# Where a decoder layer turns token-major tiles into feature-major ones: TensorE transposes, or VectorE blocks and a DMA round trip

## The chip, the cores and the metric

One core of one Trainium2 chip runs the whole kernel. The metric is the device time of one execution in microseconds (us). In the text PE is TensorE, DVE is VectorE, ACT is ScalarE, POOL is GpSimd and SP is SyncE; POOL and SP also issue DMAs, and each engine works through its own instructions in order.

## What is computed

One decoder layer on x of 256 tokens x 2048 features in float32: a half-step SwiGLU FFN (hidden width 5632), a token mixer of a gated linear attention branch (4 heads) and a dilated sliding-window attention branch (3 groups of 8 heads), merged by sigmoid gates, and a second half-step FFN. Each is modulated by shift, scale and gate rows made from a conditioning vector, and closed by a LayerNorm:

```python
f1 = swiglu(modulate(x, sh1, sc1), w_ffn1_gu[l], w_ffn1_down[l])
x = layer_norm(DN_ALPHA * x + 0.5 * g1[:, None, :] * f1, ln1_g[l], ln1_b[l])
m = hybrid_mixer(modulate(x, sh2, sc2), positions, w_in[l], w_alpha2[l], b_alpha[l],
                 gla_norm_g[l], w_branch_a[l], w_branch_b[l], w_out[l])
x = layer_norm(DN_ALPHA * x + g2[:, None, :] * m, ln2_g[l], ln2_b[l])
f2 = swiglu(modulate(x, sh3, sc3), w_ffn2_gu[l], w_ffn2_down[l])
x = layer_norm(DN_ALPHA * x + 0.5 * g3[:, None, :] * f2, ln3_g[l], ln3_b[l])
```

with, at the end of `hybrid_mixer`,

```python
y_a = o_a @ w_branch_a
...
y_b = o_b.reshape(B, S, DIL_OUT).astype(h.dtype) @ w_branch_b
merged = jax.nn.sigmoid(gate_a) * y_a + jax.nn.sigmoid(gate_b) * y_b
return merged @ w_out
```

Every product needs its left operand with the features on the partitions, while the products before it leave tokens on the partitions. So each intermediate is transposed in between.

## The kernel before

**Products.** A `Chunk` is one 512-column piece of a product for both token tiles (128 tokens each). It is cut into `Unit`s of two k-tiles (256 rows of the weight). `load` (L204) brings 4 k-tiles of a weight (1 MB, `raw`, three buffers) by SP; `split` (L209) casts a unit's part on ACT to float32r (`wh`), and `split_lo` (L220) subtracts on DVE to get the low half `wl`. `emit` (L235) issues, for both token tiles and both k-tiles, the three matmuls of `mm3` (high x high, high x low, low x high; L231 to L233) into a PSUM accumulator `acc`, 12 matmuls a unit. After a chunk's last unit it starts the chunk's `done` generator for each tile.

**The order of the work** is written out at build time. The loop at L1330 goes through all units: it splits the unit `SA` = 3 ahead, starts the generators due there, emits the unit, lets every side task of `Flow` do one step, and runs the conditioning reductions (`ada_step`, DVE, L382) up to a pace. `yield n` in a side task waits n steps. If `emit` needs a left operand whose task isn't through, `Flow.until` (L96) steps the tasks without emitting units until it is. Small SBUF tiles of 256 KB (`sml`) come from a pool of eight and are counted by `n_sml`; PSUM scratch tiles by `n_mps`.

**Left operands** are `Lhs` objects: groups kg of four feature tiles, a high and a low half, 256 tokens wide. `tok_to_lhs` (L551) fills one group for one token tile: after `wait` steps it takes a PSUM tile and makes four 128x128 transposes on PE (`transpose4`, L414), and a step later ACT copies the result to the high half (L402) and DVE subtracts to get the low half (L406). It is called

- for the FFN's hidden groups (`up_tail`, L574, wait 4): FFN1 in parts of 6 and 5 chunks, FFN2 in parts of 4, 4 and 3, each part followed by its down product, which reads the groups in order. FFN1's part 0 is "pieced": its product over the 16 k-tiles runs in five phases with partial sums in SBUF (L596, L602, L606),
- for the four heads of the linear attention (`gr_sink`, L994, into `oaT`),
- for both halves of the attention output (`lane`, L1163, into `obT`),
- for the four merged pieces (`mg_sink`, L1193, into `mT`, read by `w_out`). This sink loads `mg` from DRAM by POOL (L1198), multiplies (L1199), and adds two steps later (L1202); its chunks have four units each. `reload` (L1210) brings x back from DRAM by POOL, 1 MB per tile, at the first unit of `w_out`.

`qk_sink` (L1080) applies the rotary embedding to a q or k chunk on DVE (L1089 to L1094), transposes it on PE in the same way (L1098), and ACT copies it to `qkT` (L1101).

POOL does little else than issue DMAs: the bias rows of the conditioning, `x` for the first residual (L623), `gn`, `lng`, `lnb`, `spill`, `mgd`, `mg`.

Of the kernel before, what the change touches and what calls it, by code (L numbers as in the profile page):

```python
# [10 lines left out]
F32 = mybir.dt.float32  # L11
# [5 lines left out]
P = 128  # L17
D = 2048
S = 256
# [126 lines left out]
def layer(ctx, tc, a):  # L146
# [401 lines left out]
            yield  # L548


    def tok_to_lhs(src, lhs, kg, t, wait=2):  # L551
        yield wait
        ps = yield from mps([P, 4, P])
        transpose4(ps, src, 0)
        yield
        put_split(lhs, kg, t, ps)
        n_mps.give()

    def ffn(w_gu, w_dn, X, gm, ln, norm, parts, pieced):
# [13 lines left out]

        def up_tail(t, sg, hT, kg):  # L574
            s = sg[t]
            yield from tok_to_lhs(s, hT, kg, t, 4)
            n_sml.give()

        def up_sink(c, sg, hT, kg):
            def done(t, ps):  # L580
# [80 lines left out]

        for pi, part in enumerate(parts):
            hT = Lhs(fl)
            if pi == 0 and pieced:
                sgs = {c: [None, None] for c in part}
                for q, (k0, nk) in enumerate(PHASES):
                    if nk == 2:
                        for c in part[::2]:
                            for e in range(2):
                                it = Item(w_gu, k0 * P, e * DFF + c * NC5, True)  # L670
                                items.append(it)
                                for i in range(2):
                                    Chunk(w_gu, 0, 0, 2, X, pieced_sink(c + i, e, q, sgs[c + i], hT, c + i),
                                          k0=k0, wide=(it, i))
                    else:
                        for c in part:
                            for e in range(2):
                                Chunk(w_gu, k0 * P, e * DFF + c * NC5, nk, X,
                                      pieced_sink(c, e, q, sgs[c], hT, c), k0=k0)
            else:  # L680
                for c in part:
                    sg = [None, None]
                    kg = c - part[0]
                    Chunk(w_gu, 0, c * NC5, KD, X, gate_sink(c, sg), head=pi == 0 and c == 0)
                    Chunk(w_gu, 0, DFF + c * NC5, KD, X, up_sink(c, sg, hT, kg))
            for n in range(4):
                Chunk(w_dn, part[0] * NC5, n * NC5, 4 * len(part), hT, down_sink(pi, n), tail=pi == last and n == 3)
# [306 lines left out]
    def gr_sink(h):  # L994
# [3 lines left out]
        def done(t, ps):  # L998
            s = yield from sml(name="gr")
            A_.activation(s, ps, AF.Silu)  # L1000
            n_acc.give()
            while ("o", hh, t) not in g:
                yield
            o = g["o", hh, t]
            V.tensor_mul(o, o, s)
            n_sml.give()
            yield from tok_to_lhs(o, oaT, h, t)
            n_sml.give()
        return done

    def starter(gen, units_from):
# [65 lines left out]
    def att_set(hs4):  # L1077
        d = dict(qk={}, v={}, n=0, ob=[None, None], left=[4, 4])

        def qk_sink(which, g):  # L1080
            def done(t, ps):
# [11 lines left out]
                n_acc.give()  # L1093
                V.tensor_add(r1, r1, r2)  # L1094
                n_sml.give()
                yield 4
                pt = yield from mps([P, 4, P])
                transpose4(pt, r1.rearrange("p h e d -> p (h e d)"), 0)  # L1098
                n_sml.give()
                yield  # L1100
                A_.copy(dst[:, :, t * P:(t + 1) * P], pt)  # L1101
                n_mps.give()
                d["n"] += 1
            return done

# [57 lines left out]
        def lane(t):  # L1163
# [4 lines left out]
                yield from job(j, t)  # L1168
            while max(d["left"]):
                yield  # L1170
            yield from tok_to_lhs(d["ob"][t], obT, hs4, t)
            n_sml.give()

        for which, off in ((0, OFF_DQ), (1, OFF_DK)):
            for g in range(3):
# [17 lines left out]
    def mg_sink(n):  # L1193
        sl = slice(n * NC5, (n + 1) * NC5)

        def done(t, ps):
# [1 line left out]
            nc.gpsimd.dma_start(mg, mgd[t][:, sl])  # L1198
            V.tensor_mul(sgb[t][:, sl], sgb[t][:, sl], ps)  # L1199
            n_acc.give()  # L1200
            yield 2
            V.tensor_add(mg, mg, sgb[t][:, sl])  # L1202
            yield from tok_to_lhs(mg, mT, n, t)
            n_sml.give()
        return done

    for n in range(4):
# [161 lines left out]
```

## Time and profile before

| | us |
|---|---|
| median of 3 runs | 2717.61 (2717.35 to 2717.94) |
| profiled execution, its own time | 2717.02 |
| span of its profile | 2715.2 |
| PE busy / DVE / ACT / POOL | 2646.8 / 1925.1 / 1201.0 / 42.8 |
| mean granted clock of PE | 0.996 |

The page gives the busy time of each engine over the span, the chain of work that ended last, and the costliest groups of instructions. A busy share says how much an engine does, not whether it sets the end: that is read from the chain, from what an engine waited for, and from stretches of the span. The matmuls of one engine overlap: the record of one is 0.39 us long, and the next starts before it ends, so costs on PE are read from start to start.

### The profile page before, as it was taken

The page shows a single profiled execution, that of the slowest core. Times are in us where ns is not written, and L with a number is a line of the kernel's source. Part 1 is how long each engine was busy: PE and PEld are TensorE (multiplying, and loading weights), DVE is VectorE, ACT ScalarE, POOL GpSimd, SP SyncE. Part 2 cuts the span into 40 slices and gives each one's busy share as a digit, 9 for nine tenths or more (in the row PEclk, how much of TensorE's full clock was granted, in tenths as well). Part 3 has the DMA queues.
Part 4 walks back from the last instruction along what each step waited for, and adds up shares of the span by engine and source line. Part 5 has one row for each costly group of instructions (what it writes and reads, how often), then busy time and mean ns, then how long its engine had stood idle before and what let it go on. Part 6 is the DMA issues. An engine that isn't in the chain of part 4 may idle for free.

```text
span 2715.2 us, 31195 instructions
## 1 busy us (share of the span) xinstructions
PE 2646.8 (97%) x12043; PEld 2180.4 (80%) x12043; DVE 1925.1 (71%) x2436; ACT 1201.0 (44%) x1387; POOL 42.8 (2%) x71
## 2 busy tenths in 40 slices
PE   6899999999999999999999999999999999999997
PEld 5678788888877788888888888888788888888886
DVE  8999977877876786676666676668766655655556
ACT  5333444444345544444544344554454444443443
POOL 0000000000000000000000000000000000000001
PEclk9999999999999999999999999999999999999999
DMA  9787798888855686666657667577567666656553
GB/s 377 268 315 274 240 325 309 304 286 291 279 194 178 230 286 221 217 232 233 216 202 256 240 233 243 194 239 257 199 217 255 226 230 235 225 186 212 207 186 124
DMA packets 327044, 654.23 MB, mean 241 GB/s; under 512 B 13128, under 2 KB 21552, under 8 KB 325616
## 3 DMA queue, kind: packets, MB, share of 16 engines
q1 hardware_dynamic: 322352, 633.46, 67.0%
q0 software_dynamic: 4544, 18.79, 2.1%
q8 instruction: 94, 1.54, 0.2%
q14 instruction: 54, 0.44, 0.0%
HBM read 645.90 MB, written 6.29 MB: 240 GB/s over the span
## 4 chain that ended last, share of the span: by engine, by line
PE 87%; DVE 9%; issue 2%; ACT 1%; DMA 1%; SPq 0%; DVEq 0%; ACTq 0%
PE acc L233 27%; PE acc L232 27%; PE acc L231 27%; DVE wl L225 3%; DVE part L382 2%; PE mps L416 2%; DVE part L596 1%; PE mps L1152 1%; PE mps L1124 1%; DVE lhs L406 1%; DVE xm L424 0%; PE mps L962 0%; ACT wh L215 0%; DMA abig<-in_w_ada 0%; PE mps L1141 0%
## 5 line engine op out<-in xcount | busy, mean ns | idle before, releaser
L225 DVE TENSOR_TENSOR wl<-raw,wh 128x1024 fp32r<-128x1024 f32 x912 | 1113.3, 1223 | 697.5 <-ACT wh L215 696.1
L215 ACT CAST wh<-raw 128x1024 fp32r<-128x1024 f32 x912 | 957.4, 1053 | 1306.6 <-PE acc L233 1242.4
L231 PE MATMUL acc<-wh,lhs 128*128 128x512 f32 x3648 | 1440.0, 395 | 12.0 <-DVE part L596 7.1
L232 PE MATMUL acc<-wl,lhs 128*128 128x512 f32 x3648 | 1423.8, 390 | 5.0 <-DVE wl L225 4.9
L233 PE MATMUL acc<-wh,lhs 128*128 128x512 f32 x3648 | 1424.0, 390 | 4.6 <-DVE lhs L406 4.6
L231 PEld LDWEIGHTS acc<-wh,lhs 128*128 128x128 f32 x3648 | 686.6, 188 | 158.9 <-ACT lhs L402 7.0
L233 PEld LDWEIGHTS acc<-wh,lhs 128*128 128x128 f32 x3648 | 686.2, 188 | 150.8 <-DVE lhs L406 6.3
L232 PEld LDWEIGHTS acc<-wl,lhs 128*128 128x128 f32 x3648 | 686.6, 188 | 149.8 <-DVE wl L225 8.7
L382 DVE SCALAR_TENSOR_TENSOR part<-araw,cact,part 128x512 f32<-128x512 f32 x432 | 320.3, 742 | 0.4
L382 DVE SCALAR_TENSOR_TENSOR part<-abig,cact,part 128x512 f32<-128x512 f32 x119 | 88.1, 747 | 3.2 <-DMA abig<-in_w_ada 1.6
L596 DVE TENSOR_TENSOR part<-part,acc 128x512 f32<-128x512 f32 x72 | 46.0, 680 | 0.0
L406 DVE TENSOR_TENSOR lhs<-mps,lhs 128x512 fp32r<-128x512 f32 x64 | 41.3, 682 | 1.6 <-ACT lhs L402 1.6
L402 ACT CAST lhs<-mps 128x512 fp32r<-128x512 f32 x64 | 34.4, 585 | 0.0
L1127 DVE TENSOR_TENSOR sS<-mps,consts 128x128 f32<-128x128 f32 (+1 forms) x48 | 16.0, 358 | 15.0 <-PE mps L1124 14.5
L570 ACT ACTIVATE sg<-acc 128x512 f32<-128x512 f32 x32 | 19.0, 598 | 16.0 <-PE acc L233 16.0
L604 ACT ACTIVATE sg<-sg 128x512 f32<-128x512 f32 x12 | 7.4, 633 | 40.2 <-DVE sg L602 40.2
L406 DVE TENSOR_TENSOR lhs<-xm,lhs 128x256 fp32r<-128x256 f32 (+1 forms) x34 | 17.6, 531 | 9.2 <-ACT lhs L402 8.5
L416 PE MATMUL mps<-ident,sg 128*128 128x128 f32 x176 | 22.8, 272 | 0.0
L416 PEld LDWEIGHTS mps<-ident,sg 128*128 128x128 f32 x176 | 20.5, 140 | 2.8
L416 PE MATMUL mps<-ident,part 128*128 128x128 f32 x96 | 15.1, 281 | 7.6 <-DVE part L382 7.3
L368 POOL DMA_DIRECT2D part<-in_b_ada x12 | 5.9, 493 | 1030.8 <-DVE part L382 433.3
L1143 ACT COPY pT<-mps 128x384 f32<-128x384 f32 x24 | 10.7, 480 | 24.2 <-PE mps L1141 24.2
(221 smaller groups left out, 875.0 us busy)
## 6 DMA issues: line engine op xcount, KB each, us to landing
raw<-in_w_ffn_gu SPq DMA_DIRECT2D x176, 1024.0 KB, 4.9
raw<-in_w_in SPq DMA_DIRECT2D x152, 1024.0 KB, 4.8
araw<-in_w_ada SPq DMA_DIRECT2D x224, 512.0 KB, 5.3
raw<-in_w_ffn_down SPq DMA_DIRECT2D x88, 1024.0 KB, 5.0
abig<-in_w_ada SPq DMA_DIRECT2D x24, 1024.0 KB, 7.5
raw<-in_w_branch_a SPq DMA_DIRECT2D x16, 1024.0 KB, 5.1
raw<-in_w_out SPq DMA_DIRECT2D x16, 1024.0 KB, 6.6
raw<-in_w_branch_b SPq DMA_DIRECT2D x8, 1024.0 KB, 5.0
```

Source lines behind the costliest of these rows:

```text
L215: A_.copy(wh, r)
L225: V.tensor_sub(wl, r, wh.bitcast(F32))
L231: T.matmul(ps, lhsT=xh, rhs=wh, start=first, stop=False)
L232: T.matmul(ps, lhsT=xh, rhs=wl, start=False, stop=False)
L233: T.matmul(ps, lhsT=xl, rhs=wh, start=False, stop=last)
L382: V.scalar_tensor_tensor(pt, w, cact[:, k:k + 1], pt, op0=ALU.mult, op1=ALU.add)
L402: A_.copy(hs, src)
L406: V.tensor_sub(b[:, 1, j, t * P:(t + 1) * P], src, b[:, 0, j, t * P:(t + 1) * P].bitcast(F32))
L416: T.transpose(ps[:, j], src[:, c0 + j * P:c0 + (j + 1) * P], ident)
L596: V.tensor_add(p, p, ps)
L1124: T.matmul(ps[:, 0:nk], lhsT=qk[g][:, 0, j, t * P:(t + 1) * P], rhs=qk[g][:, 1, j, 0:nk], start=True, stop=True)
L1152: T.matmul(ops[:, 0:HD], lhsT=pTs[kb][:, g], rhs=d["v"][g][:, kb, j * HD:(j + 1) * HD], start=i == 0, stop=i == n_mm - 1)
```

## The change

A new helper `turn` makes the transpose without PE. DVE transposes the 16 blocks of 32x32 of each 128x128 tile in one instruction into a small tile `s`; four DMAs from POOL write it to a DRAM tile `turned`, each 32 partitions wide, in runs of 512 bytes, so that the blocks end up at the right places; a fifth DMA, three steps later, reads it back whole (128 rows of 2 KB) into a small tile. Three steps after that the result is used. `tok_to_lhs_dma` is `tok_to_lhs` with `turn`: ACT copies the high half and DVE subtracts the low half, now from SBUF.

It takes the place of `tok_to_lhs` for all hidden groups of an FFN part but the last, for the heads of `oaT`, for the first half of `obT` and for the first three pieces of `mT`; `qk_sink` calls `turn` too. The others stay on PE. In `mg_sink` the addition comes four steps after the product instead of two.

```diff
--- before.py
+++ after.py
@@ -548,6 +548,36 @@
             yield
 
 
+    def turn(src, wait, give):
+
+
+        yield wait
+        s = yield from sml(name="turn")
+        V.transpose(s.rearrange("p (b k j) -> p b k j", b=4, k=4), src.rearrange("p (k b j) -> p b k j", k=4, b=4))
+        if give:
+            n_sml.give()
+        d = dr.tile([P, NC5], F32, tag="turn", name="turned", bufs=6)
+        dv = d.rearrange("(b i) (a x) -> a i b x", b=4, a=4)
+        for a4 in range(4):
+            nc.gpsimd.dma_start(dv[a4], s[32 * a4:32 * a4 + 32].rearrange("i (b x) -> i b x", b=4))
+        yield 3
+        n_sml.give()
+        o = yield from sml(name="turned")
+        nc.gpsimd.dma_start(o, d)
+        yield 3
+        return o.rearrange("p (a k j) -> p k a j", a=4, k=4)
+
+    def tok_to_lhs_dma(src, lhs, kg, t, wait=1, give=True):
+        o = yield from turn(src, wait, give)
+        if kg not in lhs.tiles:
+            lhs.tiles[kg] = blk([P, 2, 4, S], F32R, name="lhs")
+        hi, lo = (lhs.tiles[kg][:, e, :, t * P:(t + 1) * P].rearrange("p k (a j) -> p k a j", a=4) for e in range(2))
+        A_.copy(hi, o)
+        V.tensor_sub(lo, o, hi.bitcast(F32))
+        lhs.ready.update(((2 * kg, t), (2 * kg + 1, t)))
+        n_sml.give()
+
+
     def tok_to_lhs(src, lhs, kg, t, wait=2):
         yield wait
         ps = yield from mps([P, 4, P])
@@ -573,8 +603,11 @@
 
         def up_tail(t, sg, hT, kg):
             s = sg[t]
-            yield from tok_to_lhs(s, hT, kg, t, 4)
-            n_sml.give()
+            if kg < hT.last:
+                yield from tok_to_lhs_dma(s, hT, kg, t)
+            else:
+                yield from tok_to_lhs(s, hT, kg, t, 4)
+                n_sml.give()
 
         def up_sink(c, sg, hT, kg):
             def done(t, ps):
@@ -661,6 +694,7 @@
 
         for pi, part in enumerate(parts):
             hT = Lhs(fl)
+            hT.last = len(part) - 1
             if pi == 0 and pieced:
                 sgs = {c: [None, None] for c in part}
                 for q, (k0, nk) in enumerate(PHASES):
@@ -1004,8 +1038,7 @@
             o = g["o", hh, t]
             V.tensor_mul(o, o, s)
             n_sml.give()
-            yield from tok_to_lhs(o, oaT, h, t)
-            n_sml.give()
+            yield from tok_to_lhs_dma(o, oaT, h, t)
         return done
 
     def starter(gen, units_from):
@@ -1093,13 +1126,9 @@
                 n_acc.give()
                 V.tensor_add(r1, r1, r2)
                 n_sml.give()
-                yield 4
-                pt = yield from mps([P, 4, P])
-                transpose4(pt, r1.rearrange("p h e d -> p (h e d)"), 0)
+                o = yield from turn(r1.rearrange("p h e d -> p (h e d)"), 1, True)
+                A_.copy(dst[:, :, t * P:(t + 1) * P].rearrange("p k (a j) -> p k a j", a=4), o)
                 n_sml.give()
-                yield
-                A_.copy(dst[:, :, t * P:(t + 1) * P], pt)
-                n_mps.give()
                 d["n"] += 1
             return done
 
@@ -1168,8 +1197,11 @@
                 yield from job(j, t)
             while max(d["left"]):
                 yield
-            yield from tok_to_lhs(d["ob"][t], obT, hs4, t)
-            n_sml.give()
+            if hs4:
+                yield from tok_to_lhs(d["ob"][t], obT, hs4, t)
+                n_sml.give()
+            else:
+                yield from tok_to_lhs_dma(d["ob"][t], obT, hs4, t)
 
         for which, off in ((0, OFF_DQ), (1, OFF_DK)):
             for g in range(3):
@@ -1198,10 +1230,13 @@
             nc.gpsimd.dma_start(mg, mgd[t][:, sl])
             V.tensor_mul(sgb[t][:, sl], sgb[t][:, sl], ps)
             n_acc.give()
-            yield 2
+            yield 4
             V.tensor_add(mg, mg, sgb[t][:, sl])
-            yield from tok_to_lhs(mg, mT, n, t)
-            n_sml.give()
+            if n < 3:
+                yield from tok_to_lhs_dma(mg, mT, n, t)
+            else:
+                yield from tok_to_lhs(mg, mT, n, t)
+                n_sml.give()
         return done
 
     for n in range(4):
```

## Rows read from the trace of the kernel before

**Rows 1.** Page, part 1: busy us (share of the span) x instructions, by engine.

```profile
PE 2646.8 (97%) x12043; PEld 2180.4 (80%) x12043; DVE 1925.1 (71%) x2436; ACT 1201.0 (44%) x1387; POOL 42.8 (2%) x71
```

**Rows 2.** Page, part 4: the chain that ended last, shares by line.

```profile
PE acc L233 27%; PE acc L232 27%; PE acc L231 27%; DVE wl L225 3%; DVE part L382 2%; PE mps L416 2%; DVE part L596 1%; PE mps L1152 1%; PE mps L1124 1%; DVE lhs L406 1%; DVE xm L424 0%; PE mps L962 0%; ACT wh L215 0%; DMA abig<-in_w_ada 0%; PE mps L1141 0%
```

**Rows 3.** Busy by stretch: us, PE, PEld, DVE, ACT, POOL, PEclk, DMA share, GB/s.

```profile
255.00:345.00 90.00, 86.07 (x391) 69.89 (x391) 84.78 (x112) 42.50 (x56) 0.97 (x2) 0.98 0.74 253
480.00:700.00 220.00, 220.00 (x1001) 182.51 (x1001) 172.84 (x205) 92.89 (x99) 3.28 (x5) 1.00 0.85 292
1120.00:1260.00 140.00, 140.00 (x646) 116.42 (x645) 99.70 (x125) 58.35 (x62) 0.00 (x0) 1.00 0.67 232
```

**Rows 4.** Waits in 262 to 345 us: us in total, times, longest.

```profile
ACT sg L604 <- DVE sg L602: 34.8, 5, 7.4
```

**Rows 5.** Timeline of DVE in 280 to 296 us: start, us, instruction.

```profile
281.57 1.28 DVE L406 TENSOR_TENSOR lhs<-mps,lhs 128x512 fp32r<-128x512 f32 x2
...
294.87 1.28 DVE L406 TENSOR_TENSOR lhs<-mps,lhs 128x512 fp32r<-128x512 f32 x2
```

**Rows 6.** Timeline of PE near 2065 us, around a group of eight transposes.

```profile
2059.63 0.39 PE L231 MATMUL acc<-wh,lhs 128*128 128x512 f32 x1
...
2064.85 0.39 PE L233 MATMUL acc<-wh,lhs 128*128 128x512 f32 x1
2065.08 1.03 PE L416 MATMUL mps<-ident,sg 128*128 128x128 f32 x8
...
2066.42 0.39 PE L233 MATMUL acc<-wh,lhs 128*128 128x512 f32 x1
```

**Rows 7.** The chain in order of time: start, us, what (a q/k group).

```profile
1141.63 0.87 PE mps L416 x8
```

**Rows 8.** Groups by line and shape: xcount, busy us, mean ns, idle before.

```profile
L380 DVE TENSOR_SCALAR part<-araw,cact 128x512 f32<-128x512 f32 x16 | 7.7, 479 | 0.0
...
L1282 DVE SCALAR_TENSOR_TENSOR x0b<-x0b,rs,lnb 128x512 f32<-128x512 f32 x2 | 3.4, 1761 | 0.0
```

**Rows 9.** Timeline of ACT and DVE at a q/k chunk, 1130 to 1155 us.

```profile
1136.23 1.06 ACT L215 CAST wh<-raw 128x1024 fp32r<-128x1024 f32 x1 [1.67 <-PE acc L233]
...
1137.66 2.35 DVE L225 TENSOR_TENSOR wl<-raw,wh 128x1024 fp32r<-128x1024 f32 x2
...
1150.73 1.05 ACT L215 CAST wh<-raw 128x1024 fp32r<-128x1024 f32 x1 [1.67 <-PE acc L233]
```

**Rows 10.** Timeline of POOL's DMA issues, and of DVE beside one of them.

```profile
357.03 1.10 POOL L623 DMA_DIRECT2D x<-in_x  x2
...
1512.31 1.14 POOL L1053 DMA_DIRECT2D mgd<-sga  x2 [42.87 <-DVE sga L1051]
...
1512.91 1.23 DVE L225 TENSOR_TENSOR wl<-raw,wh 128x1024 fp32r<-128x1024 f32 x1 [0.30 <-ACT wh L215]
```

**Rows 11.** Page, part 3, DMA queue: packets, MB, share of 16 engines' span.

```profile
q1 hardware_dynamic: 322352, 633.46, 67.0%
```

**Rows 12.** DMA issues: engine queue, xcount, KB each, median us to landing.

```profile
spill<-f POOLq DMA_DIRECT2D x2, 1024.0 KB, 5.0
mgd<-sga POOLq DMA_DIRECT2D x8, 256.0 KB, 3.3
mg<-mgd POOLq DMA_DIRECT2D x8, 256.0 KB, 5.8
...
x0b<-spill POOLq DMA_DIRECT2D x1, 1024.0 KB, 8.3
x1b<-spill POOLq DMA_DIRECT2D x1, 1024.0 KB, 11.0
```

**Rows 13.** Tile `x`: its DMAs' time to landing.

```profile
DMA to landing us min/median/max: 3.7/6.2/8.0
```

**Rows 14.** Timeline of POOL and DVE at the `mT` chunks.

```profile
1841.26 0.54 POOL L1213 DMA_DIRECT2D x0b<-spill  x1
...
1858.33 0.69 DVE L1199 TENSOR_TENSOR sgb<-sgb,acc 128x512 f32<-128x512 f32 x1 [0.67 <-PE acc L233]
```

## The prediction

> **What bounds the kernel now.** I read the page first. TensorE (PE) is busy 97% of the span, VectorE (DVE) 71%, ScalarE (ACT) 44%, GpSimd (POOL) 2% [rows 1], and the three lines of the three-term matmul carry 81% of the chain that ended last [rows 2]. The share is an average, so the stretches come next: in 480 to 700 us (second FFN1 part) and 1120 to 1260 us (q/k) PE has no idle time while DVE has 21 to 29% to spare, but in 255 to 345 us (the last phase of the pieced first FFN part) DVE is busy 84.8 of 90 us and PE is not always [rows 3]. There ACT waits 34.8 us for DVE's `sg` [rows 4]. So an edit that takes work from PE and gives it to DVE pays in most of the kernel and costs in that one stretch.
>
> A count is needed before the parts: one unit is 2 k-tiles x 2 token tiles x 3 matmuls = 12 matmuls. From 2059.63 to 2064.85 there are 23 matmul starts, 0.227 us each [rows 6], so a unit is 2.72 us. A "step" of a side task (one `yield`) is one unit while units are being emitted.
>
> **The calls that move.** FFN1: 5 chunks of part 0 and 4 of part 1, two token tiles each, 18 calls; FFN2: 3+3+2 chunks, 16; q/k: 2 x 3 x 2 chunks, 24; `oaT` 4 heads, 8; `obT` first half, 2; `mT` n<3, 6. Together 74 calls, 296 PE transposes.
>
> **What PE gets back.** A group of eight transposes (both token tiles) at 2065.08: the matmul at 2066.42 is the third after the one at 2064.85 and without the group would start 3 x 0.227 = 0.68 later, at 2065.53. So the group costs 0.89 us, 0.111 per transpose [rows 6]. The chain has the q/k groups at the same price, 0.87 [rows 7]. The 10 calls of FFN1 part 0 lie in the DVE-bound stretch and return nothing. The other 64 give 64 x 4 x 0.111 = **-28.4 us**.
>
> **What DVE gets.** One block transpose of 128x512 fp32 per call. No row shows one. The nearest rows are one-pass DVE operations of that size: 479 ns (one tensor input), 0.69 us (two tensors), and 1761 ns for the slowest [rows 8, 14]. A gain is excluded, since it is an added instruction. I take 0.69, the ordinary 512-element row. The low-half subtraction on DVE and the copy on ACT stay, one pass over 512 elements each, now from SBUF: nothing, with ACT idle more than half of the span [rows 1]. Outside FFN1 part 0 the 64 x 0.69 = 44 us hide in DVE's idle time. In q/k, the busiest place, DVE has 99.7 of 140 us [rows 3], and after a chunk its queue is late: two `wl` follow each other from 1137.66 [rows 9]. The second, made until 1140.0, moves to 1141.4 behind the two transposes; its cast began at 1136.23 [rows 9] at the start of a unit and serves the unit three later, at 1144.4, so 3 us are left. In FFN1 part 0 nothing hides it: one chunk takes 13.3 us (the `lhs` pairs at 281.57 and 294.87 [rows 5]) against 4 x 2.72 + 0.89 = 11.8 of PE. Five chunks x 2 x 0.69 = 6.9, less a little because the last low half moves out of the stretch: **+6.5 us** (4.5 at 479 ns, 17.6 at 1761 ns).
>
> **What POOL and the DMA queues get.** Five DMAs per call, 370 in all, at about 0.54 us of POOL each, the price of the pair at 1512.31 and of the pair of `x` loads [rows 10]: 200 us on an engine that is 2% busy. Bytes: 74 x 512 KB = 39 MB on 654 MB. The scatter writes rows of 512 B; I bound a packet by the 90 ns that the weight stream takes for 2 KB (67.0% of 16 x 2715 us over 322352 packets [rows 11]) and by a quarter of it: a pair's 1024 small and 256 large packets take 46 to 115 us of 16 engines, 13 to 32% of a 22 us q/k chunk whose DMA share is 0.67, and 7 to 17% of a 43 us chunk in 480 to 700 us, at 0.85 [rows 3]. The weights are three loads ahead, so I take nothing for it; at the upper end the second stretch would be full.
>
> **The new waits.** ACT's copy into the left operand now waits for a DMA that waits for another DMA. ACT is in order: behind the copy stand the casts `wh`, and behind them DVE's `wl`, and PE. Worked at the q/k chunk of [rows 9]: `wl` from 1137.66 to 1138.8, the two transposes end 1139.5 and 1140.2. POOL issues four scatters until 1141.7 and four more until 1143.9. A write to DRAM lands 3.3 us after its issue (`mgd`; 5.0 for the 1 MB `spill`), a read of 256 KB 5.8 (`mg`; 3.7 to 8.0 for `x`) [rows 12, 13]. With 3.3 + 5.8 the second tile lands at 1153.0. ACT reaches its copy seven steps after the sink, behind the cast of 1150.73 (0.9 earlier without the transposes), at 1150.9, and waits 2 us. The next cast is then 1 us late. A cast made at the start of a unit serves the unit three later, 8.2 us on, and cast plus subtraction need 2.3: 5.9 us of slack. PE stalls only if the tile lands after about 1158, that is, if the two legs together exceed 14 us. **0 us** in q/k and in the FFNs, whose chunks are as long or longer and whose DVE bursts are shorter.
>
> The exception is `mT`. Its chunks have four units, and `w_out` asks for group kg=2 at the ninth unit after chunk n=2, 8 x 2.72 = 21.8 us after its end at 1846.5 (one chunk of 11.8 us ahead of the `sgb` at 1858.33 [rows 14]): 1868.3 (times of before). The path of n=2 needs 4+1+3+3 = 11 steps, two more than there are, so the copy is called in early and simply waits. The transposes stand in DVE's queue behind the next chunk's two multiplications, which wait for that chunk's end (the same `sgb`, 0.9 earlier now): 1858.1 to 1859.5. POOL then: eight scatters to 1863.1, the two 1 MB reloads of x (program order puts them between) to 1864.2, then the reads. Before, POOL had run ahead and issued the reloads from 1841.26 [rows 14]; they landed after 8.3 and 11.0 us [rows 12]. The reads queue behind that data on the same queue, so they land near 1875.5 and PE starts kg=2 near 1876.3, 8 us late. Were they not held by the reloads, 5.8 us from 1864.7 and 1866.9 leave 2 to 4 us. Group kg=1 is within 1 us of being needed. I take **+9** (3 to 13).
>
> The Trainium skill, page "DMA: Bandwidth & Descriptors", section on the anatomy of one DMA, gives 2.0 us plus bytes over 436 GB/s for a DMA from GpSimd, that is 2.6 us for 256 KB and 6.8 for the 2 MB. The rows here are 5.8 and 11.0, so I keep the rows; by the page this stall would be some 3 us and the sum 2699.
>
> Last, POOL's small old DMAs now queue behind its waits for scatters. The x rows of the fold went out from 357.03 [rows 10], far ahead of the second FFN1 part; now they go out about when they are called, three steps (8.2 us) before use, and may stand 5 us behind a turn. With 6.2 us to land [rows 13] that is up to 3 us of DVE for two or three of eight, mostly inside the slack: **+1** (0 to 6).
>
> **Sum.** The profiled execution took 2717.0, 0.6 below the median of the runs, with 1.8 outside its span. 2717.0 - 28.4 + 6.5 + 9 + 1 = **2705**, own range 2696 to 2712.
>
> **Rivals.** *Nothing is late*: the merge reads are not held by the reloads, and the fold loads come in time: 2705 - 10 = 2695. For it: `mg` reads of 5.8 us were seen with the weight stream beside them [rows 12]; against: two steps are missing by count. *The block transpose is slow*, near 1761 ns: 17.6 instead of 6.5 in the DVE-bound stretch, 2716, no measurable change. *The round trip is too long* (the other side): DMAs of 512 B rows into DRAM and back under the weight stream take 16 us instead of 9. From 14 us on, every pair of the 24 in q/k, FFN1 part 1 and FFN2 stalls PE by the excess, here 2 us: 2705 + 48 = 2753, slower. For it: a read of 8.0 and a write of 5.0 are in the rows [rows 12, 13], 13.0 together; against: the one is a maximum, the other has 16 times the bytes of a scatter. *POOL is held by DVE*: each of a pair's eight issues waits for a DVE operation of 0.7 us, 5.6 us more, legs of 14.7, 24 x 0.6 = 14 us: 2719. The rows speak against it: the pair of issues at 1512.31 takes 1.14 us, as ever, beside a `wl` of 1.23 at 1512.91, as ever [rows 10]. The Trainium skill, page "SBUF — State Buffer", section "SBUF: two separate sides", warns of just that: a VectorE operation that uses both port pairs keeps GpSimd from writing descriptors. No run here shows whether the block transpose is such an operation.
>
> **How the numbers follow.** Forecast 0.50, nothing late 0.17, slow transpose 0.12, long round trip 0.15, POOL held 0.06. About 0.2% (5.4 us) is what a measurement of this kernel can tell from no change. Faster: the first two, 0.67. Same: the slow transpose and most of POOL held, 0.16. Slower: 0.17. The range leaves out the long round trip and the end below 2690: 2690 to 2722.
>
> **What will show it.** PE: groups of eight transposes gone, 0.89 us less between the matmuls around them from 345 us on. DVE: 74 transposes of about 0.69; chunks in 270 to 340 us 14.7 apart instead of 13.3. ACT: waits for `turned` of a few us at the copies, no PE wait behind them except one of about 8 us where `w_out` begins. I am wrong if PE waits for `lhs` after most q/k and FFN chunks, if the transposes take over 1 us, or if the `raw` loads run late.

## The result, and the profile after

| | before | after |
|---|---|---|
| median of 4 runs, us | 2717.48 (2717.19 to 2717.94) | 2748.99 (2747.22 to 2751.53) |
| span of the profiled execution | 2715.2 | 2748.3 |
| matmuls and transposes on PE | 12043 | 11747 |
| mean granted clock of PE | 0.996 | 0.989 |

The ratio is 1.0115, with a 95% interval of 1.0103 to 1.0127: 31.5 us slower, where 12 us faster had been forecast. The 296 transposes are gone from PE (12043 - 11747), and with them should have gone 28 us; some 60 us came in.

The first view is the page of after: the busy time of each engine (to be read beside [rows 1]), and the chain that ended last, by line (beside [rows 2]).

```profile
PE 2635.6 (96%) x11747; PEld 2159.1 (79%) x11747; DVE 1964.6 (71%) x2510; ACT 1202.0 (44%) x1387; POOL 246.1 (9%) x441
...
PE acc L232 23%; PE acc L233 23%; PE acc L231 23%; DVE wl L225 3%; DMA turned<-turned 2%; DMA turned<-turn 2%; DVE part L382 2%; POOL turned L562 1%; DVE part L629 1%; ACT wh L215 1%; PE mps L416 1%; PE mps L1181 1%; DVE r L1125 1%; PE mps L1153 1%; DMA raw<-in_w_in 1%
```

PE's busy time fell by only 11 us. The chain tells more: the three matmul lines that held 81% of it are down to 69%, and the write and the read of `turned` and POOL's issues, all new, have 5%. A round trip through DRAM now sets the pace somewhere. Where, the stretches of [rows 3] say. The columns are the same: us, PE, PEld, DVE, ACT, POOL, PEclk, DMA share, GB/s.

```profile
255.00:345.00 90.00, 76.87 (x316) 59.30 (x315) 82.60 (x112) 37.35 (x48) 28.47 (x52) 0.98 0.85 285
480.00:700.00 220.00, 220.00 (x985) 182.16 (x984) 179.44 (x216) 93.68 (x99) 26.26 (x47) 1.00 0.90 318
1120.00:1260.00 140.00, 132.50 (x567) 107.67 (x565) 94.93 (x123) 51.83 (x56) 29.27 (x54) 0.98 0.74 260
```

In the second FFN1 part PE is as full as before, although POOL went from 3 to 26 us there and the DMA share from 0.85 to 0.90. In q/k PE has gaps of 7.5 us in 140, where it had none.

To place the 31.5 us exactly, the two traces were laid over each other by the number of the unit: both emit the same 10944 matmuls in the same order, so the start of matmul 12 u can be compared for each unit u. This comparison is called the overlay below. After minus before, by stretch (the two profiled executions are 33.0 us apart):

| units | what runs | forecast | measured |
|---|---|---|---|
| 0 to 72 | start, first phases of FFN1 part 0 | 0 | +1.1 |
| 72 to 104 | end of FFN1 part 0 (DVE-bound) | +6.5 | +7.1 |
| 104 to 240 | FFN1 part 1, 4 groups | -3.6 | -3.6 |
| 240 to 368, 432 to 504 | fold, heads (`oaT`), `obT`, 5 groups | -4.5 + 1 | -3.1 |
| 368 to 424, 504 to 560 | the two sets of q/k, 12 groups | -10.7 | **+22.4** |
| 600 to 632 | `mT`, 3 groups | -2.7 + 9 | **+16.2** |
| 632 to 911 | FFN2, 8 groups | -7.1 | -7.0 |

All but the two bold rows came out as forecast, within about 1 us. Those hold the miss: 33.1 us in q/k and 9.9 in `mT` beyond the forecast. (Kernels below in which `mT` or q/k was not edited show by how much the two stretches vary of themselves: 12.6 to 16.2 for `mT`, 21.5 to 23.8 for q/k.)

Who waited in q/k is seen in the waits over the whole span (us in total, times, longest):

```profile
ACT qkT L1130 <- DMA turned<-turned: 65.6, 22, 5.5
ACT lhs L575 <- DMA turned<-turned: 48.2, 24, 8.9
PE acc L232 <- DVE wl L225: 30.7, 22, 2.9
```

ACT's copy waits for the read in 22 of 24 q/k tiles. That by itself need not cost PE anything: the copies into the left operands wait too, 24 times, and the FFN groups still gave 0.89 us each. But PE waits for `wl`, the operand that stands behind ACT's copy in program order. Of these 22 waits eleven, 16.7 us, lie in the two q/k stretches, and eight, 10.4 us, in FFN1 part 0. In the kernel before there were five, and none in q/k:

```profile
PE acc L232 <- DVE wl L225: 4.9, 5, 1.6
```

The loop that joins them stands whole in the chain in order of time (start, us, what):

```profile
1137.66 0.60 DVE r L1122
1138.26 0.67 DVE r L1125 x2
...
1139.57 0.71 DVE turn L556
1140.56 3.18 POOL turned L562 x6
...
1144.39 5.04 DMA turned<-turn
...
1149.96 5.72 DMA turned<-turned
...
1156.24 1.05 ACT wh L215
...
1158.46 1.22 DVE wl L225
1159.67 0.60 DVE r L1122
...
1163.57 0.71 DVE turn L556
...
1188.27 0.71 DVE turn L556
...
1215.99 0.67 DVE turn L556
```

Read it as a circle: rotary embedding on DVE (4 us for two tiles), block transpose, POOL's issues, the write, the read, then ACT's copy (at 1155.71, not listed), the cast behind it, `wl` behind the cast, and behind `wl` in DVE's queue the rotary embedding of the *next* chunk. From transpose to transpose it takes 24.0, 24.7 and 27.7 us. PE needs 8 x 2.72 = 21.8 us per chunk. So each chunk is later than the last one by 2 us or more, the slack of 5.9 us lasts for two chunks, and from the third on PE is late: for each eight units of the first set, after minus before is -0.9, -0.1, +3.0, +3.9, +1.2, +4.7, +1.0.

Two things add to the circle. Four of the stalls were followed by 3.4 us at a granted clock of 0.50, the lower of PE's two levels (1.2 GHz); here is the second of them:

```profile
1218.30:1221.70 3.40, 3.40 (x10) 2.65 (x9) 3.40 (x5) 0.00 (x0) 2.43 (x5) 0.50 0.89 248
```

By the gaps between matmul starts the four (from 1191.0, 1218.3, 1262.7 and 1627.9 us) cost 6.1 of the 33.1 us, and the stalls themselves the other 27. And in the second set the chain goes twice through a weight load that SP issued behind a late `wl` (the other is 5.91 us from 1602.14), so lateness also passes through the loads:

```profile
1632.92 9.10 DMA raw<-in_w_in
```

In `mT` the chain is another one, through POOL. It is shown with the experiments.

### The profile page after: what moved, and what is told of

Same layout as the page of the kernel before. It is cut to its first block, busy times and chain, and to the rows that moved or that the text cites. A ratio compares the mean times of both kernels' runs of the same rounds, so it can differ in the third digit from the quotient of the medians.

```text
span 2748.3 us, 31325 instructions
## 1 busy us (share of the span) xinstructions
PE 2635.6 (96%) x11747; PEld 2159.1 (79%) x11747; DVE 1964.6 (71%) x2510; ACT 1202.0 (44%) x1387; POOL 246.1 (9%) x441
## 3 DMA queue, kind: packets, MB, share of 16 engines
q1 hardware_dynamic: 322352, 633.46, 66.1%
## 4 chain that ended last, share of the span: by engine, by line
PE 73%; DVE 12%; DMA 6%; issue 5%; ACT 2%; POOL 1%; SPq 0%; DVEq 0%; ACTq 0%; POOLq 0%
PE acc L232 23%; PE acc L233 23%; PE acc L231 23%; DVE wl L225 3%; DMA turned<-turned 2%; DMA turned<-turn 2%; DVE part L382 2%; POOL turned L562 1%; DVE part L629 1%; ACT wh L215 1%; PE mps L416 1%; PE mps L1181 1%; DVE r L1125 1%; PE mps L1153 1%; DMA raw<-in_w_in 1%
## 5 line engine op out<-in xcount | busy, mean ns | idle before, releaser
L562 POOL DMA_DIRECT2D turned<-turn x296 | 161.9, 555 | 1206.2 <-DVE turn L556 1194.8
L566 POOL DMA_DIRECT2D turned<-turned x74 | 41.3, 559 | 166.7 <-DMA turned<-turn 138.7
L576 DVE TENSOR_TENSOR lhs<-turned,lhs 128x512 fp32r<-128x512 f32 x50 | 33.3, 688 | 27.0 <-ACT lhs L575 26.9
L575 ACT CAST lhs<-turned 128x512 fp32r<-128x512 f32 x50 | 30.5, 619 | 48.3 <-DMA turned<-turned 48.2
L1130 ACT COPY qkT<-turned 128x512 f32<-128x512 f32 x24 | 14.9, 621 | 65.6 <-DMA turned<-turned 65.6
L1156 DVE TENSOR_TENSOR sS<-mps,consts 128x128 f32<-128x128 f32 (+1 forms) x48 | 16.0, 358 | 14.8 <-PE mps L1153 14.4
L600 ACT ACTIVATE sg<-acc 128x512 f32<-128x512 f32 x32 | 18.9, 597 | 14.2 <-PE acc L233 14.2
L416 PE MATMUL mps<-ident,part 128*128 128x128 f32 x96 | 15.3, 284 | 8.3 <-DVE part L382 7.9
```

Source lines behind the costliest of these rows:

```text
L416: T.transpose(ps[:, j], src[:, c0 + j * P:c0 + (j + 1) * P], ident)
L562: nc.gpsimd.dma_start(dv[a4], s[32 * a4:32 * a4 + 32].rearrange("i (b x) -> i b x", b=4))
L566: nc.gpsimd.dma_start(o, d)
L575: A_.copy(hi, o)
L576: V.tensor_sub(lo, o, hi.bitcast(F32))
```

## The experiments

Three theories stood for q/k. *Loop*: the round trip is in a circle with the next chunk's rotary embedding, and the circle takes longer than PE's chunk. *Plain lateness*: each copy comes a few us late, and each step of room takes that much off. *Contention*: the 512-byte packets and POOL's issues slow the weight stream or DVE, and the waits are only where it shows.

**More steps between the read and the copy.** The only edit is the number of steps between the read's issue and the copy of a q/k tile: 3 in the changed kernel, and 4, 6 and 5 here.

```diff
-    def turn(src, wait, give):
+    def turn(src, wait, give, last=3):
...
-        yield 3
+        yield last
         return o.rearrange("p (a k j) -> p k a j", a=4, k=4)
...
-                o = yield from turn(r1.rearrange("p h e d -> p (h e d)"), 1, True)
+                o = yield from turn(r1.rearrange("p h e d -> p (h e d)"), 1, True, 4)
```

> Only the q/k sinks differ from the changed kernel: their copy comes four steps after the read is issued, not three. Loop theory: in the changed kernel the twelve q/k chunks go in a loop (rope on VectorE, block transposes, eight issues on GpSimd, write, read, ScalarE's wait and cast, VectorE's subtraction, next rope) of 24 to 28 us where TensorE needs 21.8, and cost 21.4 us against the kernel before where they should have given back 10.7. One step later the copy stands behind the next chunk's rope, the loop loses the rope (4 us) and is shorter than 21.8: all 32 us come back, 2717 us (2714 to 2722). Plain lateness (each chunk is late by itself, no loop): one step takes 2.7 us off each wait of some 3 to 6 us, about half of the stalls stay: 2730 to 2738. Contention (the added DMAs and VectorE work as such slow the weight stream and TensorE): no change, 2749.

Measured 2736.78 (2735.01 to 2737.64), ratio 1.0068 (1.0053 to 1.0083). That is the time of plain lateness, not the 2717 of the loop. The trace says why: the circle was not opened. The copy is called one step later, but the next rotary embedding still stands behind a cast and a `wl` that are queued after the copy; only one of the two `wl` that stood between them is out. This is its chain:

```profile
1162.24 0.71 DVE turn L556
...
1172.98 5.54 DMA turned<-turned
...
1179.07 1.05 ACT wh L215
1180.14 1.23 DVE wl L225
1181.37 0.60 DVE r L1122
...
1185.27 0.72 DVE turn L556
```

The circle is 23.0 us here, still over 21.8. So the theory stood, but what I had taken for its cut was not one, and this run alone could not tell it from plain lateness.

> Only the q/k sinks differ: copy six steps after the read is issued. Loop theory and plain lateness: no ScalarE wait is left in q/k, 2717 us (2714 to 2722), and TensorE 0.89 us shorter per q/k chunk than in the kernel before. Contention: 2749 or near.

Measured 2714.42 (2712.97 to 2716.62), ratio 0.9987 (0.9978 to 0.9997). Every q/k group gives 0.89 us back, and all that q/k lost is regained. Two theories remain, which differ in the number between.

> The read of a q/k tile is issued five steps after its block transposes instead of three, two steps (5.4 us of units) more room between the issue of the writes and ACT's copy; all else as in the changed kernel. Loop theory, as mended after the run with one more step: lateness carries over because ACT's copy stands ahead of the cast whose low half stands on DVE ahead of the next chunk's rope. It is gone as soon as the copy stands behind the cast that the next rope's predecessor needs; two steps more should do that for nearly every chunk: 2749 - 32 to -27, that is 2717 to 2722. Plain lateness (each step of room takes off about the same): one step gave 12 and three gave 34.6, so two give about 23: 2724 to 2728.

(This text puts the two steps ahead of the read; the edit puts them behind it. The room for the copy is the same.) Measured 2714.68 (2712.30 to 2714.95), ratio 0.9987 (0.9977 to 0.9997). In the two q/k stretches the overlay has +22.4 us with three steps, +11.4 with four, -10.7 with five and -10.7 with six: the first step gave 11, the second 22, the third nothing. If each chunk were late by itself, a further step could give no more than the one before it; a circle that is opened at the second step looks like this. The timelines of ACT and DVE show it. First the changed kernel, at the first chunk's second tile, ACT's rows and then DVE's:

```profile
1155.71 0.62 ACT L1130 COPY qkT<-turned 128x512 f32<-128x512 f32 x1 [4.30 <-DMA turned<-turned]
1156.24 2.95 ACT L215 CAST wh<-raw 128x1024 fp32r<-128x1024 f32 x3
...
1157.31 2.36 DVE L225 TENSOR_TENSOR wl<-raw,wh 128x1024 fp32r<-128x1024 f32 x2 [4.66 <-ACT wh L215]
1159.59 0.68 DVE L1122 TENSOR_TENSOR r<-acc,cosf 128x512 f32<-128x512 f32 x1
```

and the kernel with five steps:

```profile
1154.78 1.05 ACT L215 CAST wh<-raw 128x1024 fp32r<-128x1024 f32 x1 [1.67 <-PE acc L233]
1155.74 1.14 ACT L1130 COPY qkT<-turned 128x512 f32<-128x512 f32 x2
...
1155.87 1.22 DVE L225 TENSOR_TENSOR wl<-raw,wh 128x1024 fp32r<-128x1024 f32 x1 [1.50 <-ACT wh L215]
1157.01 0.68 DVE L1122 TENSOR_TENSOR r<-acc,cosf 128x512 f32<-128x512 f32 x1
```

The second tile's copy is made at about the same time in both, 1155.7 and 1156.3. But in the second kernel the cast that the next rotary embedding needs stands *ahead* of the copies, and the embedding starts at 1157.0 instead of 1159.6. Its block transposes then stand at 1139.23, 1160.99 and 1182.75, 21.76 us apart: PE's own pace. Shown, then: what counted here was on which side of one cast the copy stands. The round trip was not shorter in the second kernel: from this tile's block transpose to the landing of its read it took 16.3 us, against 15.5 in the changed one.

**The price of q/k, and the traffic by itself.** In the first of two kernels q and k are transposed on PE as before the change, the rest stays changed. The second adds to it the block transposes, the scatters and the read of every q/k tile, whose result nobody uses.

```diff
-                o = yield from turn(r1.rearrange("p h e d -> p (h e d)"), 1, True)
-                A_.copy(dst[:, :, t * P:(t + 1) * P].rearrange("p k (a j) -> p k a j", a=4), o)
+                yield 4
+                pt = yield from mps([P, 4, P])
+                transpose4(pt, r1.rearrange("p h e d -> p (h e d)"), 0)
                 n_sml.give()
+                yield
+                A_.copy(dst[:, :, t * P:(t + 1) * P], pt)
+                n_mps.give()
```

> The q/k sinks transpose on TensorE as before, all else as in the changed kernel. All theories: what q/k costs against the kernel before goes away, 2749 - 21 = 2728 us; it prices the q/k part alone and is the base for the next kernel.

Measured 2729.25 (2727.43 to 2729.70), ratio 1.0040 (1.0025 to 1.0055); by the overlay each q/k chunk takes what it took in the kernel before, to 0.02 us.

> The q/k sinks transpose on TensorE as before, and beside that make the block transposes on VectorE, the four writes and the read, whose result nobody uses or waits for. Loop theory: the traffic is free, within 3 us of the kernel with q/k on TensorE alone, 2728 to 2731. Contention: the 32 us are the price of the traffic, so 2745 to 2760.

Measured 2725.91 (2723.15 to 2726.78), ratio 1.0029 (1.0018 to 1.0039). With all of the traffic and none of the waits, the stretch from 1110 to 1300 us is full. This is the row of the windows of that kernel (columns as above):

```profile
1110.00:1300.00 190.00, 190.00 (x870) 157.85 (x869) 140.01 (x176) 81.91 (x88) 38.33 (x70) 1.00 0.78 273
```

PE has no idle time and the same 870 matmuls as without the traffic, with POOL busy for 38 us beside it. Contention by itself is out; the price of q/k comes with the waits. (The second kernel's median is 3.3 us below the first's. The profiled executions are 1.9 us apart, and that lies outside q/k: from DVE's last instruction to the end of the span the first needed 8.2 us and most others 4.4, for the landing of the output.)

**`mT`.** Two rivals: the reads are held by the reloads of x, as forecast, or the steps that are missing and POOL's own queue make them late. First the price, then the reloads alone.

```diff
-            yield 4
+            yield 2
             V.tensor_add(mg, mg, sgb[t][:, sl])
-            if n < 3:
-                yield from tok_to_lhs_dma(mg, mT, n, t)
-            else:
-                yield from tok_to_lhs(mg, mT, n, t)
-                n_sml.give()
+            yield from tok_to_lhs(mg, mT, n, t)
+            n_sml.give()
```

> The three merged pieces n<3 go back to TensorE transposes, with the addition two steps after the product as before; the rest is the changed kernel. By the starts of the matmuls the merge region cost +16.2 us against the kernel before, so 2749 - 16 = 2733 (2731 to 2735). Rival: the region inherits its lateness from the q/k chunks and oaT/obT before it, and part of the loss stays: 2738 to 2745.

Measured 2735.55 (2734.89 to 2736.52), ratio 1.0066 (1.0051 to 1.0081): 13.4 us less. From unit 600 to 632 the overlay has 0.0 instead of +16.2; 2.5 us of the difference were given back at the very end, where this kernel's profiled execution took 6.9 us from DVE's last instruction to the end of the span instead of 4.4.

```diff
-    starter(lambda: reload(), m)
+    starter(lambda: reload(), m - 12)
```

> The two 1 MB reads of x are issued 12 units (33 us) earlier, so they are not ahead of the merge reads on POOL's queue; the merged pieces still take the DRAM round trip. If the reads of n=2 are held by the reloads: the 10.8 us stall at group kg=2 falls to about 3 or 4 and the stretch at the lower clock level shrinks with it: -8 to -13, 2736 to 2741. If the steps that are missing by count and POOL's lateness are the cause: 2745 to 2749. The reloads now run beside the weights of w_branch_b, which costs nothing if those stay three loads ahead.

Measured 2744.27 (2741.54 to 2750.86), ratio 1.0101 (1.0086 to 1.0116). This interval overlaps that of the changed kernel, and the four executions lie between 2741.5 and 2750.9, so the time settles little. The trace, of an execution of 2742.0, says more: from unit 600 to 632 the loss is 9.0 us instead of 16.2, and below the 12.6 that was the least in any trace in which `mT` was not edited. Neither theory had it all. PE's waits from 1850 to 1960 us, the changed kernel first and then this one:

```profile
PE acc L231 <- ACT lhs L575: 13.1, 2, 9.7
```

```profile
PE acc L231 <- ACT lhs L575: 8.9, 3, 5.7
```

The longest falls by 4 us. Most of the rest of the difference is the clock, which cost 4.5 us in the first kernel and 1.2 in the second. In the changed kernel the windows of 5 us around the longest wait are:

```profile
1910.00:1915.00 5.00, 0.00 (x0) 0.00 (x0) 1.05 (x2) 0.00 (x0) 0.55 (x1) 0.62 1.02 422
1915.00:1920.00 5.00, 1.35 (x3) 1.11 (x4) 1.04 (x2) 1.62 (x3) 0.00 (x0) 0.50 1.02 407
1920.00:1925.00 5.00, 5.00 (x13) 3.84 (x13) 2.20 (x4) 1.41 (x3) 0.00 (x0) 0.52 0.45 148
1925.00:1930.00 5.00, 5.00 (x23) 4.09 (x23) 2.45 (x2) 1.28 (x2) 0.00 (x0) 1.00 0.02 9
```

PE stood from its last transposes near 1909 to 1918.65 and came back at a granted clock of 0.50, the lower of its two levels (1.2 GHz): 13 matmuls in 5 us instead of 22. Fourteen gaps between matmul starts of 0.43 us (the first 0.59) instead of 0.227 are 3.0 us lost after the data was there, and 1.5 more were lost in the same way after the shorter wait that began at 1896.3. The DMA share of 1.0 in the first two windows is the reloads' 2 MB beside the weights.

What still was late is seen in the chain of the changed kernel, at the pieces:

```profile
1877.26 6.11 DMA turned<-turn
...
1884.03 0.56 POOL turned L566
...
1885.10 6.18 DMA mg<-mgd
...
1891.56 5.37 DMA turned<-turn
...
1897.50 0.56 POOL turned L566
...
1898.58 6.72 DMA mg<-mgd
```

POOL waits for the first piece's write before it can issue the read; behind the read stand the next piece's `mg` loads; and scatters wait for `mg` loads that they don't use, as POOL's timeline shows:

```profile
1884.57 1.07 POOL L1230 DMA_DIRECT2D mg<-mgd  x2
1885.63 3.29 POOL L562 DMA_DIRECT2D turned<-turn  x6
1889.73 0.55 POOL L562 DMA_DIRECT2D turned<-turn  x1 [0.81 <-DMA mg<-mgd]
1891.56 0.55 POOL L562 DMA_DIRECT2D turned<-turn  x1 [1.28 <-DMA mg<-mgd]
```

The seventh and the eighth scatter were issued when the first and the second `mg` load, eight issues before, had landed. Eight DMAs seem to be all that POOL had under way at once; in the whole trace there are never more between issue and landing. Why, no run shows. From the second read of one piece to that of the next POOL takes 13.5 us (1884.03 to 1897.50), and PE's chunk is 4 x 2.72 = 10.9: a second circle, through POOL.

It was tried in two steps. The first gives the two missing steps back, on top of the early reloads:

```diff
-            yield 4
+            yield 2
             V.tensor_add(mg, mg, sgb[t][:, sl])
```

> As the run with the two reads of x issued 12 units earlier, and besides the merge's addition comes two steps after the product again, as before the change, so the path of a piece needs nine steps, as many as there are. That run had lost its hold by the reloads and still stalled 5.7 us at group kg=2 and 3.2 at the others. If the missing two steps (5.4 us) are the rest: both stalls fall to 0 or 1 and the time by 8 to 9 against that run, 2735 to 2737. If the rest is POOL's issues standing behind each other and behind its DMAs: little change, 2742 to 2745.

Measured 2742.24 (2739.36 to 2742.71), ratio 1.0087 (1.0072 to 1.0102); from unit 600 to 632 the loss is 8.4 us instead of 9.0. As long as POOL issues the `mg` loads, the steps that my count had missing are worth next to nothing. The wait only changed its place. This is DVE's in 1850 to 1925 us:

```profile
DVE mg L1234 <- DMA mg<-mgd: 13.7, 5, 3.9
```

DVE is now called early to the addition and waits for `mg`, which POOL issued behind the eight scatters of the piece before (4.4 us of issues, 4.5 to 7.2 to land). So the last run leaves all that and lets ACT issue the `mg` loads:

```diff
-            nc.gpsimd.dma_start(mg, mgd[t][:, sl])
+            nc.scalar.dma_start(mg, mgd[t][:, sl])
```

> As the run with the reads of x early and the merge's addition after two steps (2742.2), but the four pairs of mg loads are issued by ACT instead of POOL. In that run the chain went round a second loop: block transposes, eight scatters on POOL, the next piece's mg load behind them (issue to landing 5.6 to 7.2 us), the addition, the next block transposes; DVE waited 13.7 us for mg. If POOL's order is the cause, this loop is gone: DVE's wait for mg falls below 3 us, PE's stalls of 7.9 us there to those of one round trip that is too long for its 21.8 us by up to 4 us: 2731 to 2738. If the landings under the weight stream are the cause whatever the queue: 2741 to 2744.

Measured 2736.91 (2734.53 to 2738.91), ratio 1.0067 (1.0050 to 1.0083), 5.3 us less than the run before it, and 4.0 us instead of 8.4 from unit 600 to 632. DVE's wait for `mg` in 1850 to 1925 us is down from 13.7 us to this:

```profile
DVE mg L1234 <- DMA mg<-mgd: 1.4, 1, 1.4
```

So the place behind POOL's other DMAs was its cause. What is left seems to be the round trip itself: ACT still waits 15.3 us for `turned` in that stretch. No run tested it.

**FFN1 part 0.** All five groups back on PE (`hT.first` marks the pieced part).

```diff
-            if kg < hT.last:
+            if kg < hT.last and not hT.first:
...
+            hT.first = pi == 0 and pieced
```

> The five hidden groups of FFN1's pieced part 0 go back to TensorE transposes; the rest is the changed kernel. The stretch is bound by DVE, the ten block transposes are in DVE's chain and the PE transposes in its gaps, so all of the +7.1 us measured there comes back: 2749 - 7 = 2742 (2741 to 2743). Rival: PE becomes the bound again by 10 x 4 x 0.111 = 4.4 us and only 2 to 3 us come back: 2746.

Measured 2741.13 (2737.33 to 2741.21), ratio 1.0083 (1.0068 to 1.0098): 7.9 us less. The whole price comes back, so PE's transposes are free in that stretch and DVE's are not.

**All three mends together**: six steps for q/k, `mT` and FFN1 part 0 on PE.

> Three mends together: the q/k reads issued six steps after the block transposes, the merged pieces back on TensorE, FFN1's part 0 back on TensorE. If the parts are independent, as the starts of the matmuls say, the sum is 2714.4 (q/k mended alone) - 13.4 (what the merge run gave) - 7.9 (what the part 0 run gave) = 2693, faster than both kernels. By the terms of the prediction: 2717.5 less 54 calls x 4 x 0.111 = 24.0, with no other price: 2693.5. Rival: something carries over from one part to the other as it did between q/k chunks, and the gains overlap: 2698 or more.

(In the edit the q/k copies stand six steps behind the issue of the read, as in the run with six steps. And 54 is a wrong count: 74 calls less 6 in `mT` and 10 in FFN1 part 0 are 58, so by the terms of the prediction 2717.5 - 25.8 = 2691.7.) Measured 2693.44 (2692.02 to 2694.14), ratio 0.9908 (0.9891 to 0.9924): 24.6 us faster than the kernel before. By the overlay of the changed kernel the three mends are worth 33.1 + 16.2 + 7.1 = 56.4, that is 2692.6: the parts add up. PE has 11811 instructions, 232 transposes fewer than before, and the chain by engine is:

```profile
PE 85%; DVE 10%; issue 2%; ACT 2%; DMA 1%; SPq 0%; DVEq 0%; ACTq 0%
```

> As the run with the three mends, but the first merged piece alone (n = 0, which has the time of three more chunks before it is read) keeps the DRAM round trip: two calls more without PE transposes. If a piece with that much room is free: 0.9 us less than that run, which the measurement can hardly tell. If POOL's queue or the reload holds it back as it did the other pieces: 1 to 4 us more.

Measured 2692.97 (2692.08 to 2694.19), ratio 0.9908 (0.9893 to 0.9923). The time can't tell the two apart; by the starts of the matmuls the first piece gives its 0.89 us.

## Why the prediction was wrong

- **PE's 0.111 us per transpose: right.** Wherever PE is the bound and nothing is late, a group of eight gives 0.89 us back, to two hundredths (FFN1 part 1, most groups of FFN2, and q/k as soon as the circle is open). The 232 transposes that the kernel with the three mends no longer makes should give 25.8 by this; 24.6 were measured.
- **The block transpose at 0.69 us, and +6.5 in FFN1 part 0: right.** The line's 74 instructions have medians of 686 to 705 ns by tile; the stretch lost 7.1 us, and the run with part 0 on PE got it back. The five pairs of transposes stand at 270.56 to 329.88, 14.8 us apart on average, where [rows 5] have 13.3 and I forecast 14.7.
- **Nothing for the traffic: right.** POOL's issues take 0.555 us each. The traffic without the waits costs no PE time, and the weights' median landing time rose from 4.9 to 5.5 us. Issues beside a block transpose took 0.57 us, the others 0.55, so the rival in which DVE holds POOL is out. One sign of being wrong did come, loads of `raw` that are late: the casts waited six times, 18.9 us in all, for mixer weights, and before never. With five steps they still waited four times, 7.2 us, and q/k lost nothing, so the late loads alone don't explain the loss.
- **"0 us in q/k": the step that failed.** Its legs were near in the first chunk: the write took 5.0 instead of 3.3 us, the read 5.7 as assumed, together 10.8 of the 14 us that I gave as the limit. The limit itself was wrong. I worked the slack of 5.9 us for one chunk that starts on time, and asked whether its lateness reaches PE. I did not ask whether it reaches the next chunk's block transposes, though I had written down the link: behind the copy stand the casts `wh`, behind them DVE's `wl`, and DVE's queue holds the next rotary embedding as well. The right limit is one for a circle: embedding, transposes, issues, write, read, cast and `wl` together must be under 21.8 us, or the copy must stand behind the cast that the next embedding follows. From the trace of before the sum could be made: from the embedding's start to the end of the second tile's issues an estimate of 4 + 1.4 + 4.4 of work, then 3.3 + 5.8 + 0.5, then 2.3 to 3.5 for cast and `wl`: some 21.7 to 22.9 us, at the limit even with the short legs that I took, and over it with the 5.0 that the write needed. That sum was not made. What the runs showed in place of the 0 is +22.4 us in the two q/k stretches, where -10.7 had been forecast.
- **The rival "round trip too long" had the right time for the wrong reason.** It gave 2753 from 2 us of excess at each of 24 pairs, in the FFNs too. In FFN1 part 1 and FFN2 nothing was lost; a hidden group there has two chunks of time, 43 us, to the next, which may be why, but no run tested it. What q/k lost came from 12 pairs that passed their lateness on.
- **`mT` +9: the mechanism right in one part, the size wrong.** A read behind the reloads took as long as forecast (10.2 us for the one issued at 1907.74). But I took POOL's issues as free but for their 0.54 us. In fact POOL waits, in order, for each write ahead of its read, and for `mg` loads it doesn't need, so everything began later; and the clock fell after the longest wait. The stalls came to 13.4 us and the clock with a short wait for the low half to 5.3, against 9 in all.
- **The missing steps: not borne out.** Calling the addition two steps earlier gave 0.6 us on top of the early reloads, since it then waited for `mg`. What the steps are worth when ACT issues those loads, no run shows.
- **The fold's x loads, +1: rather low.** The fold, the heads and `obT` together came to -3.1 against -3.5 with that term, and to -1.8 to -3.1 in the traces of the other kernels. So 1.3 to 2.7 us of the 4.5 were lost there; which of the three has the loss was not followed further.

With q/k mended alone, the kernel takes 2714.4, and the forecast of 2705 is off by 9.4 us. Nearly all of that is `mT`, where this kernel lost 14.7 us by its overlay and 6.3 had been forecast.

The Trainium skill, page "VectorE: DVE Perf Modes", sections "The three transpose paths" and "Rules for kernel authors", says to make a 128x128 transpose on TensorE if its result may go to PSUM, and that VectorE's covers blocks of 32x32 only. By that rule none of the 74 calls should move. The runs agree for FFN1 part 0 and for `mT`, where the move cost 7.9 and 13.4 us, and differ for the rest: 58 calls that have 0.1 us of PE for each transpose and time for the detour give 24.6 us.

The Trainium skill, page "DMA: Bandwidth & Descriptors", section "Anatomy of one DMA — SWDGE (gpsimd) path", gives 2.0 us plus bytes over 436 GB/s, which makes 2.2 us for a scatter of 64 KB and 2.6 for the read. The medians here are 4.6 and 5.6, with the weights beside them. As an estimate from that page's figures, the circle in q/k would be about 6 us shorter than its 24.0, below PE's 21.8, and would have cost nothing; the measurement decides.

## What to carry to other kernels

When a result comes back by a longer way, don't ask only whether the slack of one tile covers it: follow what stands behind the waiting instruction on its engine until you come back to the next tile's start, and compare the time of that circle with the bound's pace. If the circle is too long, move the consumer behind the instruction on which the next tile hangs, for two steps were worth 34 us here. An engine that issues DMAs and waits for them in order is a pipeline stage too, with a time per tile of its own, and loads that others wait for are better issued elsewhere, as `mg` by ACT here (5.3 us).

## What the runs showed of the hardware

- A 64 KB write of 512-byte rows from POOL took 4.6 us (median of 296) and a 256 KB read 5.6 (median of 74, 2.8 to 10.2) from issue to landing, with the weight stream beside them.
- Transposes between other matmuls cost PE 0.111 us each in its stream, though their record of eight is 1.03 us long [rows 6]; the block transposes of four such tiles, one instruction on DVE, took 0.69.
- The DMAs from POOL moved 57.6 MB and took 6.0% of the 16 engines' span, beside 66.1% for the weights. In the kernel with the traffic and without its waits the q/k matmuls kept their pace to 0.02 us a chunk.
- After PE had stood for some 10 us in `mT` it ran at the lower clock level (0.50) for about 6 us of matmuls, a price of 3.0 us on top of the wait. After four stalls in q/k, with gaps between matmul starts of 2.0 to 3.3 us, it did so for 3.4 us each, 6.1 us in all; after others of that length it did not.
- POOL never had more than eight DMAs under way in the changed kernel; in the merge the ninth was issued when the first had landed. This is read from the trace and was not tried by itself.
